# Router to first expert unit: normed tokens kept by feature column, their bf16 parts cut behind the first unit's columns, the gate row behind up

## The chip, the cores and the metric

The kernel runs on one core of a Trainium2 chip. The metric is the device time of one execution in microseconds (us). The engines named below are TensorE (PE: matmul; PEld: its weight loads), VectorE (DVE), ScalarE (ACT), GpSimd (POOL) and SyncE (SP), which here only issues DMA transfers. In tile names, `p_...` tiles lie in PSUM, the others in SBUF.

## The reference

Two transformer blocks on 256 tokens of 1024 features, one after the other, in float32. The place of the change is the mixture of experts at the end of the first block:

```python
h = rms_norm(x, g_ffn[l]) * (1.0 + scale_f) + shift_f
# hierarchical_moe(h): t = h as (256, 1024)
g_logits = t @ w_group + b_group                  # 4 groups
g_sel = argmax(g_logits)
e_logits = (t @ w_router[g_sel]) + b_router       # 8 experts of the chosen group
top_v, top_i = top_k(e_logits, 2)
w_top = softmax(top_v) * p_group
comb = sum(one_hot(eid, 32) * w_top)              # 256 x 32
hg, hu = t @ w_gate[e], t @ w_up[e]               # 32 experts, 1024 -> 256
y = sum over e of (silu(hg) * hu * comb[:, e]) @ w_down[e]
x = x + gate_f * y
```

## The kernel before, in words

The 256 tokens lie in two tiles t = 0, 1 of 128 partitions (`xt`, 1024 features each). Features are dealt out over partitions so that feature 8p + j belongs to column j; eight columns j = 0..7 make up one token.

The router (written out by hand, lines 1017 to 1050) goes tile by tile: `square` and `rstd` make 1/rms; `normed` (line 950) writes the normed tokens `xn2` (called `xn` in the profile) on ACT; `turned` copies the transposed tokens out of PSUM; `logits`, `groups` and `experts` find the two experts of each token (`selb`); `rank` and `places` count the tokens of an expert up to a slot number and make the 0/1 matrix `P0` (`P` in the profile). `gather_t` (line 998) then multiplies column j of `xn2` by `P0`, 8 float32 matmuls for each t, which moves the tokens of the first four experts into their slots (`p_xg`). Two kinds of order hold there: while the list `holding` is not empty, what goes through `held` keeps the order in which it is written, and with two entries so do matmuls. `warm(n)` issues n matmuls whose result nobody reads.

The 32 experts are worked off in 8 units of 4. A unit reads its gathered tokens `xg` (from `p_xg`, scaled on DVE and ACT by turns, `gather`, line 1059), multiplies by the gate and up weights (`gate_up`, `p_gu`), applies silu, and multiplies by the down weights (`p_dn`), which are scattered back (`p_sc`). While unit k runs, `prepare(k + 1)` gathers the tokens of the next one, in three bf16 parts instead of float32: `cut3` (line 1008) cuts the two tiles of `xn2` into `xn3` (also `xn` in the profile), with two ACT and two DVE passes over 1024 elements for each tile. `cut3` overwrites `xn2` on the way. Before the change these passes were not held: a scheduler places them.

`gate_row_end` (line 369) spreads one row over all partitions with two 512-wide matmuls (`p_row`); nobody needs it before the first unit's `p_dn` is read.

Expert weights, 1 MB each, come over SP's queue in a fixed order into rings of buffers (`load_experts`, line 228). `xn2` itself lies in the first of the five buffers of the ring `raw3`, so the load of that buffer's next owner, and all loads queued behind it, wait until `cut3` has read `xn2` for the last time:

```python
xn2 = raw3.tile([128, RAW], FT, name="xn2", tag="raw3")
```

Units 1 to 6 end in a branch (`branch`, `tc.If`, the profile's L1302) on the largest count of the unit; all engines pass through it, and SP's loads behind it are issued after it.

Of the kernel before, what the change touches and what calls it, by code (L numbers as in the profile page):

```python
# [11 lines left out]
AF = mybir.ActivationFunctionType  # L12
OP = mybir.AluOpType
# [19 lines left out]
def tile_block(ctx: ExitStack, tc: tile.TileContext, A, out):  # L33
    nc = tc.nc
    pe, act, dve, pool = nc.tensor, nc.scalar, nc.vector, nc.gpsimd
# [10 lines left out]
    def bank(shape, name):  # L46
        return ps.tile(shape, FT, name=name, tag="bank")
# [26 lines left out]
    holding = []  # L74

    def held(ins):

        if holding:
            tc.keep_in_program_order(ins)
        return ins  # L80
# [14 lines left out]
    def held_pe(ins):  # L95
        if len(holding) > 1:
            tc.keep_in_program_order(ins)

    def mm(o, lhsT, rhs, start, stop):
        held_pe(pe.matmul(o, lhsT, rhs, start=start, stop=stop, skip_group_check=True))  # L100

    def warm(n):

        if n:
            p = bank([128, 128], "p_warm")
            for _ in range(n):
                tc.keep_in_program_order(
                    pe.matmul(p, ident, ones, start=True, stop=True, skip_group_check=True))
# [27 lines left out]
    xt = const.tile([128, 2, D], FT, name="xt")  # L136
# [70 lines left out]
    for name in 'bq bq bk 2 2 bk bv bv 3 aq kv 2 2 3 3 aq 3 4 4 4 4 5 5 5 5'.split():  # L207
        if name == "kv":
            w_kv = load_cols("wkv", "w_in", WIN, 512, 256, 0, 8)
        elif name in COLS:  # L210
            c0, n = COLS[name]
            k = len(later[name])
# [156 lines left out]
    def gate_row_end():  # L369
        m = modrow[:, 1]  # L370
        b = [bank([128, 512], "p_row") for _ in range(2)]
        for half in range(2):
            mm(b[half], ones, m[:, 512 * half:512 * half + 512], True, True)
        for half in range(2):
            act.activation(m[:, 512 * half:512 * half + 512], b[half], AF.Copy)
# [75 lines left out]
    af = const.tile([128, 8], FT, name="af")  # L451
# [4 lines left out]
    bf_ = modcol[:, 2]  # L456
# [107 lines left out]
    def add_out(t, half):  # L564
        add_outs[0](t, half)
# [267 lines left out]
    st = proj_fm(w_iq, iqT, 1.0)  # L833
# [75 lines left out]
    xn2 = raw3.tile([128, RAW], FT, name="xn2", tag="raw3").rearrange("p (t d) -> p t d", t=2)  # L909
# [11 lines left out]
    rs2 = m1.tile([128, 2], FT, name="rs2")  # L921
# [7 lines left out]
    xn3 = m1.tile([128, 3, 2, 8, 128], BF, name="xn3")  # L929
# [13 lines left out]
    def rstd(t, step):  # L943
# [3 lines left out]
        else:  # L947
            held(dve.reciprocal(rs2[:, t:t + 1], ss2[:, t, 1:2]))

    def normed(t):  # L950
        held(act.activation(xn2[:, t], xt[:, t], AF.Copy, scale=rs2[:, t:t + 1]))

    def turned(t, half):
        if half:
            held(act.activation(xh[t][1], trb[t][1], AF.Copy))
        else:
            held(dve.tensor_copy(xh[t][0], trb[t][0]))
# [26 lines left out]
    def rank(t):  # L984
        if t:
            mm(pos_[:, 1], oneb, selb[:, 0], False, False)
        mm(pos_[:, t], trib, selb[:, t], t == 0, True)

    def places(t):
        held(dve.scalar_tensor_tensor(pos1[:, t], pos_[:, t], 1.0, selb[:, t], op0=OP.add, op1=OP.mult))  # L990
        held(dve.tensor_tensor(P0[:, t], iota1[:, None, 0:SLOTS].to_broadcast([128, 4, SLOTS]),
                               pos1[:, t, 0:4, None].to_broadcast([128, 4, SLOTS]), op=OP.is_equal))

    PP, XG = {}, {}
    P0f = P0.rearrange("p t e s -> p t (e s)")
    xgb = [bank([128, 4, 128], "p_xg") for _ in range(2)]

    def gather_t(t):
        for j in range(8):
            mm(xgb[j // 4][:, j % 4], xn2[:, t, j::8], P0f[:, t], t == 0 and j % 4 == 0, t == 1)  # L1000

    def gather_mm(u, banks, t):
        for j in range(8):
            for i in range(3):
                mm(banks[j // 4][:, j % 4], xn3[:, i, t, j], PP[u][:, t],
                   t == 0 and j % 4 == 0 and i == 0, t == 1 and i == 2)

    def cut3(src, parts):

        act.activation(parts[0], src, AF.Copy)  # L1010
        dve.tensor_tensor(src, src, parts[0], op=OP.subtract)
        act.activation(parts[1], src, AF.Copy)
        dve.tensor_tensor(parts[2], src, parts[1], op=OP.subtract)

    holding += [True, True]
    square(0, 0)
# [2 lines left out]
    rstd(0, 1)  # L1019
    add_out(1, 0)  # L1020
    turned(0, 0)
    normed(0)
    turned(0, 1)
    add_out(1, 1)
    logits(0)
    trb.append(turn_x(1))
# [11 lines left out]
    rank(0)  # L1038
    warm(3)
    places(0)  # L1040
    gather_t(0)
    warm(2)
    groups(1)
    experts(1)
    rank(1)
    places(1)
    warm(0)
    gather_t(1)
    del holding[:]
    def onehot(u, pos, slot):  # L1050

        n = pos.shape[2]
        P = m1.tile([128, 2, 4, SLOTS], BF, name="Pq", tag="Pq", bufs=3)[:, :, 0:n]
        for t in range(2):
            dve.tensor_tensor(P[:, t], slot[:, None, :].to_broadcast([128, n, SLOTS]),
                              pos[:, t, :, None].to_broadcast([128, n, SLOTS]), op=OP.is_equal)
        PP[u] = P.rearrange("p t e s -> p t (e s)")

    def gather(u, banks=None):

        n = 4 * SLOTS
        xg = m1.tile([128, 8, 128], FT, name="xg", tag="xg", bufs=XGB)[:, :, 0:n]
        if not banks:
            banks = [bank([128, 4, 128], "p_xg")[:, :, 0:n] for _ in range(2)]
            for t in range(2):
                gather_mm(u, banks, t)
        for jq in range(2):
            b = banks[jq]
            for jj in range(4):
                j = 4 * jq + jj  # L1070
                if jj % 2:
                    act.activation(xg[:, j], b[:, jj], AF.Identity, bias=bf_[:, j:j + 1], scale=af[:, j:j + 1])  # L1072
                else:
                    dve.tensor_scalar(xg[:, j], b[:, jj], af[:, j:j + 1], bf_[:, j:j + 1],  # L1074
                                      op0=OP.mult, op1=OP.add)
        XG[u] = xg

    gather(0, xgb)
    onehot(0, pos1[:, :, 0:4], iota1[:, 0:SLOTS])
    for t in range(2):  # L1080
        cut3(xn2[:, t].rearrange("p (n j) -> p j n", j=8), [xn3[:, i, t] for i in range(3)])


    p = bank([128, NEXP], "p_cnt")
# [41 lines left out]
    def gate_up(st, k):  # L1126
        if k == "g":
            st.b = bank([128, 512], "p_gu")
        o = 0 if k == "g" else 256
        for j in range(8):  # L1130
            for c, e in enumerate(st.es):
                s0 = SLOTS * c
                mm(st.b[SLOTS * c:SLOTS * c + SLOTS, o:o + 256], XG[st.u][:, j, s0:s0 + SLOTS], W[e, k][:, j],
                   j == 0 and o == 0, j == 7)
# [17 lines left out]
    def silu(st):  # L1152
        st.s = m1.tile([128, 256], FT, name="sl", tag="sl")
        act.activation(st.s[:st.n], st.b[:st.n, 0:256], AF.Silu)  # L1154
        dve.tensor_tensor(st.s[:st.n], st.s[:st.n], st.b[:st.n, 256:512], op=OP.mult)  # L1155
# [138 lines left out]
    def prepare(u):  # L1294
        es = ORDER[u]
        onehot(u, pos1[:, :, es[0]:es[0] + 4], iota1[:, 0:SLOTS])
        gather(u)
# [18 lines left out]
    for u, es in enumerate(ORDER):  # L1316
        st = Unit()
        st.u, st.es, st.n, st.y = u, es, SLOTS * len(es), {}
        units.append(st)
    for k, st in enumerate(units):  # L1320
        free = 0 < k < nu - 1
        n = len(st.es)
        gate_up(st, "g")
        if not free:
            load_experts(n)
        gate_up(st, "u")
        if not free:
            load_experts(n)
        silu(st)
        if k == 0:  # L1330
            gate_row_end()
        if k == 3:
            fallback()
        if k < nu - 1:
            prepare(k + 1)
        slots(st)
        turn(st)
        if st is not units[-1]:
            down(st)
            if not free:  # L1340
                load_experts(n)
            scatter(st)
            if free:
                branch(st)
                load_experts(3 * n)
        if k == 0:
            gr = modrow[0:24, 0, 0:128]
            for i, n in enumerate(("g_final", "mix_norm_w_2", "ffn_norm_w_2")):
                pool.dma_start(gr[8 * i:8 * i + 8], dram(n, 0, [[128, 8], [1, 128]]))
        if k == 2:  # L1350
            lb, oml, sp8 = constants2()
            p = bank([128, 24], "p_gg")
            pe.transpose(p, gr, ident[:24, :24])
            gcols = const.tile([128, 24], FT, name="gcols")
            dve.tensor_copy(gcols, p)
            gg = const.tile([128, 8], FT, name="gg")
            dve.tensor_mul(gg, gcols[:, 0:8], gcols[:, 8:16])
            nr = norm_row(0, "g_final")
        if 2 <= k <= 5:
            next(nr)  # L1360
# [62 lines left out]
    st = fm2(w_f, lambda b: fbanks.extend(b), (0,1,))  # L1423
# [27 lines left out]
    for fg in range(11):  # L1451
        src = [[2 * DFF, 128], [128 * 2 * DFF, 8], [1, 256]]
# [406 lines left out]
    st = gate_up2(0)  # L1859
# [53 lines left out]
    for half in range(2):  # L1913
# [10 lines left out]
                                  op0=OP.mult, op1=OP.mult))  # L1924
# [31 lines left out]
```

## Time and profile before

| | us |
|---|---|
| median of 3 runs (730.46 to 731.74) | 730.86 |
| the profiled execution's own time | 731.0 |
| its span, first to last instruction | 729.3 |
| PE busy / DVE busy / ACT busy | 661.0 / 400.2 / 303.5 |
| mean granted TensorE clock | 0.966 of full speed |

The profile records one execution. Some 1.7 us of its time lie outside the span. Times of rows are us from the start of the span. The router's last part and the first unit lie between 176 and 221 us, the eight units end at about 416 us, and the second block follows.

### The profile page before, as it was taken

The page shows a single profiled execution, that of the slowest core. Times are in us where ns is not written, and L with a number is a line of the kernel's source. Part 1 is how long each engine was busy: PE and PEld are TensorE (multiplying, and loading weights), DVE is VectorE, ACT ScalarE, POOL GpSimd, SP SyncE. Part 2 cuts the span into 40 slices and gives each one's busy share as a digit, 9 for nine tenths or more (in the row PEclk, how much of TensorE's full clock was granted, in tenths as well). Part 3 has the DMA queues.
Part 4 walks back from the last instruction along what each step waited for, and adds up shares of the span by engine and source line. Part 5 has one row for each costly group of instructions (what it writes and reads, how often), then busy time and mean ns, then how long its engine had stood idle before and what let it go on. Part 6 is the DMA issues. An engine that isn't in the chain of part 4 may idle for free. (4 is left out here: it accounts for less than half of the span.)

```text
span 729.3 us, 13242 instructions
## 1 busy us (share of the span) xinstructions
PE 661.0 (91%) x5489; PEld 511.3 (70%) x5489; DVE 400.2 (55%) x753; ACT 303.5 (42%) x505; POOL 46.1 (6%) x71
## 2 busy tenths in 40 slices
PE   4799999999899776898696999999999999999996
PEld 1498787677745524445252499987899999898994
DVE  2367967877653221323312378879576555555555
ACT  1446454754541101101110286775465444444445
POOL 7010000001000000000000153100000000000001
PEclk9899999999899998999987999999999999999998
DMA  9999669996469899998999999633535555550001
GB/s 343 372 381 375 233 262 337 378 420 218 175 273 421 328 417 416 359 423 328 421 421 412 372 364 391 220 117 116 174 116 175 196 200 196 172 202 17 1 1 58
DMA packets 69202, 196.93 MB, mean 270 GB/s; under 512 B 7550, under 2 KB 33219, under 8 KB 57350
## 3 DMA queue, kind: packets, MB, share of 16 engines
q1 hardware_dynamic: 67558, 195.30, 70.8%
q8 instruction: 53, 0.87, 0.5%
q10 hardware_dynamic: 1216, 0.30, 0.2%
q0 software_dynamic: 352, 0.28, 0.1%
q14 instruction: 23, 0.19, 0.1%
HBM read 194.81 MB, written 1.05 MB: 269 GB/s over the span
## 5 line engine op out<-in xcount | busy, mean ns | idle before, releaser
L100 PE MATMUL p_gu<-Xl,wguh 128*128 128x256 f32 x352 | 99.8, 284 | 0.0
L100 PE MATMUL p_gu<-Xh,wgul 128*128 128x256 f32 x352 | 99.3, 283 | 0.0
L100 PE MATMUL p_gu<-Xh,wguh 128*128 128x256 f32 x352 | 98.9, 283 | 0.1
L100 PEld LDWEIGHTS p_gu<-Xl,wguh 128*128 128x128 f32 x352 | 67.5, 192 | 0.5
L100 PEld LDWEIGHTS p_gu<-Xh,wguh 128*128 128x128 f32 x352 | 67.1, 192 | 0.7 <-ACT Xh L1385 0.4
L100 PEld LDWEIGHTS p_gu<-Xh,wgul 128*128 128x128 f32 x352 | 67.4, 192 | 0.3 <-DVE wgul L87 0.2
L100 PE MATMUL p_gu<-eg,xg 128*32 128x256 f32 x576 | 43.9, 434 | 16.6 <-PEq L1302 9.2
L100 PEld LDWEIGHTS p_gu<-eg,xg 128*32 128x32 f32 x576 | 21.1, 123 | 37.9 <-issue 26.8
L87 DVE TENSOR_TENSOR wdnl<-wdn,wdnh 128x1024 fp32r<-128x1024 f32 x22 | 27.0, 1225 | 32.4 <-ACT wdnh L86 32.4
L1155 DVE TENSOR_TENSOR sl<-sl,p_gu 128x256 f32<-128x256 f32 x9 | 3.8, 421 | 71.0 <-ACT sl L1154 71.0
L1154 ACT ACTIVATE sl<-p_gu 128x256 f32<-128x256 f32 x9 | 3.5, 383 | 89.4 <-PE p_gu L100 89.4
L100 PE MATMUL p_w<-hTh,wih 128*128 128x256 f32 x128 | 37.7, 298 | 2.5 <-ACT wih L86 2.5
L87 DVE TENSOR_TENSOR wgul<-wup,wguh 128x1024 fp32r<-128x1024 f32 x22 | 27.0, 1225 | 21.3 <-ACT wguh L86 20.2
L86 ACT ACTIVATE wdnh<-wdn 128x1024 fp32r<-128x1024 f32 x22 | 23.3, 1058 | 36.5 <-PE p_gu L100 35.9
L1072 ACT ACTIVATE xg<-p_xg,modcol,af 128x128 f32<-128x128 f32 x36 | 15.5, 460 | 54.1 <-DVE xg L1074 53.8
L87 DVE TENSOR_TENSOR wgul<-wgt,wguh 128x1024 fp32r<-128x1024 f32 x22 | 26.9, 1225 | 19.8 <-ACT wguh L86 19.8
L100 PE MATMUL p_dn<-ed,aT 128*32 128x512 f32 (+2 forms) x304 | 33.1, 573 | 4.9 <-ACT aT L1162 4.9
L100 PE MATMUL p_w<-Xh,w2h 128*128 128x256 f32 x128 | 37.0, 289 | 0.5 <-ACT w2h L86 0.3
L86 ACT ACTIVATE wguh<-wgt 128x1024 fp32r<-128x1024 f32 x22 | 23.3, 1061 | 33.7 <-PE p_gu L100 18.2
L100 PE MATMUL p_w<-hTl,wih 128*128 128x256 f32 x128 | 37.0, 290 | 0.0
L100 PE MATMUL p_w<-hTh,wil 128*128 128x256 f32 x128 | 36.7, 291 | 0.0
L100 PE MATMUL p_w<-Xh,w2l 128*128 128x256 f32 x128 | 36.1, 284 | 0.6 <-DVE w2l L87 0.6
(624 smaller groups left out, 1591.0 us busy)
## 6 DMA issues: line engine op xcount, KB each, us to landing
eg<-in_w_gate_dram SPq DMA_DIRECT2D x32, 1024.0 KB
eu<-in_w_up_dram SPq DMA_DIRECT2D x32, 1024.0 KB
ed<-in_w_down_dram SPq DMA_DIRECT2D x28, 1024.0 KB
wada<-in_w_ada_dram SPq DMA_DIRECT2D x24, 1024.0 KB
w<-in_w_in_dram SPq DMA_DIRECT2D x11, 1024.0 KB
wgt<-in_w_gate_up_dram SPq DMA_DIRECT2D x11, 1024.0 KB
wup<-in_w_gate_up_dram SPq DMA_DIRECT2D x11, 1024.0 KB
wdn<-in_w_down_dram SPq DMA_DIRECT2D x11, 1024.0 KB
```

The source lines that it names most:

```text
L86: held(act.activation(hi, src, AF.Copy))
L87: held(eng.tensor_tensor(lo, src, f32(hi), op=OP.subtract))
L100: held_pe(pe.matmul(o, lhsT, rhs, start=start, stop=stop, skip_group_check=True))
L1072: act.activation(xg[:, j], b[:, jj], AF.Identity, bias=bf_[:, j:j + 1], scale=af[:, j:j + 1])
L1154: act.activation(st.s[:st.n], st.b[:st.n, 0:256], AF.Silu)
L1155: dve.tensor_tensor(st.s[:st.n], st.s[:st.n], st.b[:st.n, 256:512], op=OP.mult)
```

## The change

The normed tokens are stored column by column: `xnj` is `xn2` seen as (t, j, n), and `normed` now reads `xt` with a step of 8 elements and writes each column in one piece. `gather_t` and `cut3` then read pieces without a step. `turned(0, 1)` goes ahead of `normed(0)`. `gather_t(0)` is split: columns 0 to 5 ahead of the second tile's group and expert choice, columns 6 and 7 behind its rank; the two `warm(2)` matmuls go (the third call issued none). The evictions `xg` are held in the order of j, and `cut3` is held behind them in two steps, over both tiles each. In unit 0, matmuls are held too, and `gate_row_end` goes behind the up product.

```diff
+    xnj = xn2.rearrange("p t (j n) -> p t j n", j=8)
+
     def normed(t):
-        held(act.activation(xn2[:, t], xt[:, t], AF.Copy, scale=rs2[:, t:t + 1]))
+        held(act.activation(xnj[:, t], xt[:, t].rearrange("p (n j) -> p j n", j=8), AF.Copy,
+                            scale=rs2[:, t:t + 1]))
-    def gather_t(t):
-        for j in range(8):
-            mm(xgb[j // 4][:, j % 4], xn2[:, t, j::8], P0f[:, t], t == 0 and j % 4 == 0, t == 1)
+    def gather_t(t, js):
+        for j in js:
+            mm(xgb[j // 4][:, j % 4], xnj[:, t, j], P0f[:, t], t == 0 and j % 4 == 0, t == 1)
-    def cut3(src, parts):
-        act.activation(parts[0], src, AF.Copy)
-        dve.tensor_tensor(src, src, parts[0], op=OP.subtract)
-        act.activation(parts[1], src, AF.Copy)
-        dve.tensor_tensor(parts[2], src, parts[1], op=OP.subtract)
+    def cut3(src, parts, step):
+        if step == 0:
+            held(act.activation(parts[0], src, AF.Copy))
+            held(dve.tensor_tensor(src, src, parts[0], op=OP.subtract))
+        else:
+            held(act.activation(parts[1], src, AF.Copy))
+            held(dve.tensor_tensor(parts[2], src, parts[1], op=OP.subtract))
...
     turned(0, 0)
+    turned(0, 1)
     normed(0)
-    turned(0, 1)
...
-    gather_t(0)
-    warm(2)
+    gather_t(0, range(6))
     groups(1)
     experts(1)
     rank(1)
+    gather_t(0, range(6, 8))
     places(1)
-    warm(0)
-    gather_t(1)
-    del holding[:]
+    gather_t(1, range(8))
...
     gather(0, xgb)
+    for step in range(2):
+        for t in range(2):
+            cut3(xnj[:, t], [xn3[:, i, t] for i in range(3)], step)
+    del holding[:]
     onehot(0, pos1[:, :, 0:4], iota1[:, 0:SLOTS])
-    for t in range(2):
-        cut3(xn2[:, t].rearrange("p (n j) -> p j n", j=8), [xn3[:, i, t] for i in range(3)])
...
+        if k == 0:
+            holding += [True, True]
         gate_up(st, "g")
...
         gate_up(st, "u")
...
-        silu(st)
         if k == 0:
             gate_row_end()
+            del holding[:]
+        silu(st)
```

In `gather`, the two eviction calls are wrapped in `held` and are otherwise as before.

The order on DVE at the second tile's expert choice, before (`selb` is the choice, `pos` and `P` the slots; `xn_1884` is `xn2`, `xn_1910` is `xn3`):

```order
L981 MATCH_REPLACE gone<-top_243,le_1897 128x32
L1011 TENSOR_TENSOR xn_1884<-xn_1884,xn_1910 128x8x128
L982 TENSOR_SCALAR selb<-gone 128x32
L990 SCALAR_TENSOR_TENSOR pos_1902<-p_pos,selb 128x32
L1088 COPY counts<-p_cnt 128x32
L991 TENSOR_TENSOR P_1914<-iota_1898,pos_1902 128x128
```

and after the change:

```order
L985 MATCH_REPLACE gone<-top_243,le_1897 128x32
L986 TENSOR_SCALAR selb<-gone 128x32
L994 SCALAR_TENSOR_TENSOR pos_1902<-p_pos,selb 128x32
L995 TENSOR_TENSOR P_1914<-iota_1898,pos_1902 128x128
```

The first pass of `cut3` no longer stands between the search and the choice. Where the passes stand now, on DVE, behind the evictions `xg` (`sl` is unit 0's silu product):

```order
L1080 TENSOR_SCALAR xg<-p_xg,af,modcol 128x128 x2
L1115 CAST comb_2058<-le_1897 128x64
L1116 TENSOR_TENSOR crest<-le_1897,comb_2058 128x64
L1080 TENSOR_SCALAR xg<-p_xg,af,modcol 128x128
L1117 CAST comb_2058<-crest 128x64
L1118 TENSOR_TENSOR comb_2058<-crest,comb_2058 128x64
L1016 TENSOR_TENSOR xn_1884<-xn_1884,xn_1910 128x1024 x2
L1019 TENSOR_TENSOR xn_1910<-xn_1884,xn_1910 128x1024 x2
L1164 TENSOR_TENSOR sl<-sl,p_gu 128x256
```

All four DVE passes follow one another between the last eviction and the silu product. On PE, from the first gather to the first unit, before:

```order
L100 MATMUL p_xg<-P_1914,xn_1884 128x128 x8
L108 MATMUL p_warm<-ones,ident 128x128 x2
...
L100 MATMUL p_pos<-selb,trib 128x32
L100 LDWEIGHTS oneb
L100 MATMUL p_cnt<-selb,oneb 128x32
L100 MATMUL p_xg<-P_1914,xn_1884 128x128 x8
L100 MATMUL p_gu<-eg,xg 32x256 x8
L100 MATMUL p_row<-modrow,ones 128x512 x2
L100 MATMUL p_gu<-eg,xg 32x256 x24
L100 MATMUL p_gu<-eu,xg 32x256 x32
```

and after:

```order
L100 MATMUL p_xg<-P_1914,xn_1884 128x128 x6
...
L100 MATMUL p_pos<-selb,trib 128x32
L100 MATMUL p_xg<-P_1914,xn_1884 128x128 x2
L100 LDWEIGHTS oneb
L100 MATMUL p_cnt<-selb,oneb 128x32
L100 MATMUL p_xg<-P_1914,xn_1884 128x128 x8
L100 MATMUL p_gu<-eg,xg 32x256 x32
L100 MATMUL p_gu<-eu,xg 32x256 x32
L100 MATMUL p_row<-modrow,ones 128x512 x2
```

Two of the first gather's products moved behind the rank, and the row's two products moved from inside the gate product to behind up. A float32 matmul of these rows stands in the profile as two instructions.

## Rows read from the trace of the kernel before

**Rows 1.** The page, part 2: mean DMA busy tenths, 40 slices of the span.
```profile
DMA  9999669996469899998999999633535555550001
```

**Rows 2.** Windows: stretch, us, busy of PE, PEld, DVE, ACT, POOL, PEclk, DMA, GB/s.
```profile
190.00:194.00 4.00, 2.18 (x15) 1.98 (x14) 2.21 (x4) 0.90 (x4) 0.00 (x0) 1.00 0.00 0
194.00:198.00 4.00, 3.46 (x14) 3.49 (x15) 3.30 (x9) 1.81 (x2) 0.00 (x0) 0.71 0.00 0
206.00:236.00 30.00, 28.83 (x386) 15.98 (x379) 10.19 (x24) 5.07 (x15) 0.00 (x0) 1.00 0.99 407
236.00:244.00 8.00, 4.92 (x38) 2.41 (x40) 3.56 (x7) 0.00 (x0) 0.00 (x0) 0.97 0.56 208
242.00:408.00 166.00, 132.49 (x1511) 70.17 (x1511) 40.86 (x86) 17.50 (x46) 1.02 (x2) 0.91 0.97 396
```

**Rows 3.** Waits of SP's queue: total us, times, longest us.
```profile
SPq L252 <- PEq L1302: 48.9, 4, 17.9
SPq L252 <- DVE xn L1013: 25.1, 1, 25.1
```

**Rows 4.** Timeline of SP: start, us, what.
```profile
205.46 1.94 SPq L252 DMA_DIRECT2D ed<-in_w_down_dram  x4
...
241.92 1.92 SPq L252 DMA_DIRECT2D ed<-in_w_down_dram  x3
```

**Rows 5.** Timeline of DVE and PE, second tile's choice and gather: idle in brackets.
```profile
189.49 0.18 DVE L981 MATCH_REPLACE8 gone<-top,le 128x32 f32<-128x32 f32 x1
...
191.52 2.00 DVE L1011 TENSOR_TENSOR xn<-xn,xn 128x1024 f32<-128x1024 f32 x1 [1.85 <-PE p_xg L100]
...
193.43 0.18 DVE L982 TENSOR_SCALAR selb<-gone 128x32 bf16<-128x32 f32 x1
...
194.10 0.29 DVE L991 TENSOR_TENSOR P<-iota,pos 128x128 f32<-128x128 f32 x1
...
194.54 4.17 PE L100 MATMUL p_xg<-P,xn 128*128 128x128 f32 x16 [0.68 <-DVE P L991]
```

**Rows 6.** Weight loads by tile (ns min/median/max), and a run of warm matmuls.
```profile
L100 PEld LDWEIGHTS p_xg<-P,xn x32: 313/336/341, 187.4 to 198.1; 128*128 128x128 f32 x32
...
L100 PEld LDWEIGHTS p_lg<-wr,h x32: 186/192/333, 179.3 to 186.4; 128*128 128x128 f32 x32
...
186.56 0.91 PE L108 MATMUL p_warm<-ones,ident 128*128 128x128 f32 x6
```

**Rows 7.** Lines by form, 160 to 212 us: count, busy us, mean ns.
```profile
L1010 ACT ACTIVATE xn<-xn 128x1024 bf16<-128x1024 f32 x2 | 4.2, 2094 | 0.0
L86 ACT ACTIVATE woh<-woa 128x1024 fp32r<-128x1024 f32 x3 | 3.2, 1064 | 3.6 <-PE p_wo L100 3.6
L951 ACT ACTIVATE xn<-xt,rs 128x1024 f32<-128x1024 f32 x2 | 2.3, 1142 | 0.2 <-DVE rs L948 0.2
...
L1013 DVE TENSOR_TENSOR xn<-xn,xn 128x1024 bf16<-128x1024 f32 x2 | 4.1, 2046 | 1.8 <-ACT xn L1012 1.8
L87 DVE TENSOR_TENSOR wol<-woa,woh 128x1024 fp32r<-128x1024 f32 x3 | 3.6, 1209 | 0.0
L1074 DVE TENSOR_SCALAR xg<-p_xg,af,modcol 128x128 f32<-128x128 f32 x5 | 1.9, 407 | 1.9 <-PE p_xg L100 1.9
```

**Rows 8.** Timeline, first unit: gate, row, up, next unit's gather.
```profile
198.64 1.27 PE L100 MATMUL p_gu<-eg,xg 128*32 128x256 f32 x16
...
199.84 1.98 PE L100 MATMUL p_row<-modrow,ones 128*128 128x512 f32 x4
...
203.60 2.37 PE L100 MATMUL p_gu<-eg,xg 128*32 128x256 f32 x40 [1.21 <-ACT xg L1072]
...
205.21 0.42 DVE L1103 SCALAR_TENSOR_TENSOR le<-le,w,selb 128x32 f32<-128x32 f32 x2
...
205.78 3.64 PE L100 MATMUL p_gu<-eu,xg 128*32 128x256 f32 x64
...
209.35 2.85 PE L100 MATMUL p_xg<-Pq,xn 128*128 128x128 bf16 x48
```

More of the change, by code (lines that the diff above doesn't have):

```diff
@@ L1071, in gather @@
                 if jj % 2:
-                    act.activation(xg[:, j], b[:, jj], AF.Identity, bias=bf_[:, j:j + 1], scale=af[:, j:j + 1])
-                else:
-                    dve.tensor_scalar(xg[:, j], b[:, jj], af[:, j:j + 1], bf_[:, j:j + 1],
-                                      op0=OP.mult, op1=OP.add)
+                    held(act.activation(xg[:, j], b[:, jj], AF.Identity, bias=bf_[:, j:j + 1],
+                                        scale=af[:, j:j + 1]))
+                else:
+                    held(dve.tensor_scalar(xg[:, j], b[:, jj], af[:, j:j + 1], bf_[:, j:j + 1],
+                                           op0=OP.mult, op1=OP.add))
         XG[u] = xg
     gather(0, xgb)
+    for step in range(2):
+        for t in range(2):
+            cut3(xnj[:, t], [xn3[:, i, t] for i in range(3)], step)
+    del holding[:]
     onehot(0, pos1[:, :, 0:4], iota1[:, 0:SLOTS])
-    for t in range(2):
-        cut3(xn2[:, t].rearrange("p (n j) -> p j n", j=8), [xn3[:, i, t] for i in range(3)])
     p = bank([128, NEXP], "p_cnt")
```

## The prediction

> **What bounds the kernel now.** I read the page's slices first. DMA falls to four tenths in the slice around 190 us [rows 1]; the windows resolve that: no byte moves from 190 to 198 us, the engine stays nearly fully supplied from 206 to 236, dips in 236 to 244, and runs at 0.97 over 242 to 408 [rows 2]. So the expert units are bound by transfers once they run, and the router's end is a stretch where transfers stand still. The waits of SP's queue say why: one wait of 25.1 us on DVE's L1013, the last pass that reads `xn2`, whose buffer the next load needs, and later waits on the branch L1302 [rows 3]. SP issues again at 205.46, and after the first unit's branch at 241.92 [rows 4]. The time in question is therefore the shift of that restart at 242: transfers are idle just ahead of it in either kernel, and what follows hangs on it.
>
> What sets 242? SP waits there for PE to arrive at the branch. From the second unit's gather at 209.35 to the branch PE runs 28.83 of 30 us [rows 2, 8], on weights that landed before 190 or come with the loads of 205. So the shift of the gather at 209.35 is the gain, as long as the transfers can follow: they restart at 205.46, and have 8 x (1 - 0.56) = 3.5 us of idle time to give ahead of 242 [rows 2, 4].
>
> **The change part by part.** Each step moves the start of that gather.
>
> (a) DVE. The search ends at 189.67, but `selb` starts at 193.43: the first `cut3` pass stands between, waits 1.85 us for PE to finish reading `xn2` (it overwrites it) and runs 2.00 [rows 5]. Now `selb` follows at once: -3.7 us. PE must be free for the rank at 189.9: the first gather starts at about 187.4, and six columns are 12 instructions; at 0.15 us (below) they end at 189.2, at the old 0.26 (4.17 / 16) at 190.5. With `P` 3.7 earlier, the second gather starts at 190.84 instead of 194.54.
>
> (b) The gather itself. Its 16 instructions took 4.10 us to the first `p_gu` at 198.64 [rows 5, 8]. Their weight loads, with a step of 8 elements, take 336 ns; those of `p_lg`, without one, 192; six warm matmuls of the same size run in 0.91, 0.15 each [rows 6]. I take 0.15 for loads without a step: 2.4 us, -1.7. Bounds: 0.26, no gain; and 0.12, an estimate for the warm run without the drain of its last product, 0.5 more. I take 0.15 because the warm run has the same form (128 x 128, float32, no step), and 192/336 of 0.26 is 0.15 too.
>
> [...]
>
> (c) The gate product. From the first `p_gu` to the next gather 10.71 us pass now [rows 8]; in them lie the row product, and waits for evictions that stand behind `cut3` passes on DVE and ACT. Steady `p_gu` needs 3.57 us for 64 instructions (205.78 to 209.35), 7.14 for gate and up. Now the evictions come first: column 0 starts at about 192.5, an estimate (its bank is complete at 192.05, eight instructions into the gather, and DVE has slot work of 0.2 us each until then), column 1 on ACT is ready by 193.4; before column 2 stand five small DVE operations at 0.2 us (0.42 for two), so it is ready at 194.3; the later ones, at 0.41 each and two pairs of small ones, keep ahead of PE's 0.45 a column. PE starts at 190.84 + 2.4 = 193.24, loses 0.2 to column 2, and ends up at 200.58. That is 7.34 instead of 10.71, -3.4.
>
> (d) The row product now adds to PE: four instructions, 199.84 to 201.75 before, where it lay in a wait [rows 8]: +1.9. The gather starts at 202.5.
>
> (e) `cut3`. Its last eviction is done at 196.0. Eight passes in pairs: with ACT at 1.06 and DVE at 1.21 (without a step) [rows 7], the chain ACT, DVE, ACT, DVE with the two tiles staggered ends at 201.9, 0.6 ahead of the gather: cost nothing while PE works through up and row. No row shows a bf16 pass without a step at this size; the other end is today's 2.05, which ends it at 206.3 (a rival). Silu's ACT work stands behind it, ready by 202, ahead of need.
>
> SP's load then goes out at 202.0, 3.5 us earlier. With the 3.5 us of idle time the transfers can follow 7.0.
>
> (f) `normed` reads with a step: from 1142 ns to at most 2094 [rows 7]. On ACT each of its two runs is followed today by a `cut3` pass of 2094 ns, which goes away there, so ACT is 1.1 us earlier behind each, not later. The tokens are first read at 187.4 and 190.8. Hidden, cost nothing; without that cover it would be 0.95 a tile on the second tile's path. `turned(0, 1)` moves ahead of it, on work that PE has finished: nothing.
>
> (g) The warm matmuls: PE would have waited there anyway; nothing, apart from the clock (a rival).
>
> Sum: -3.7 - 1.7 - 3.4 + 1.9 = -6.9 us. The profiled execution took 731.0 (its span 729.3 and 1.7 around it), so 724.1; the median of the runs is 0.14 below that execution, which gives 724.0. The likeliest case's own range is 1.2 either way: rank and eviction order by 0.3 each, the gather's speed by 0.6, and states of the clock further on.
>
> **The rivals.**
>
> *The gather does not run faster.* Then the rank waits for PE until 190.5, the second gather starts at about 191.7 and runs 4.1; `p_gu` finds its evictions ready, 7.14, row 1.9: the next gather at 204.85, gain 4.5, 726.4. For: p_lg's form differs. Against: [rows 6].
>
> [...]
>
> *`cut3` stays at 2.05 us a pass* because of bf16 and not the step. It ends at 206.3; the gather gains 3.0, SP's load goes out 0.9 us later than now, and the transfers gain 3.5 - 0.9 = 2.6: 728.3.
>
> *Slower: `cut3` in series.* If ACT and DVE did not overlap over the two tiles (held in order, at 2.05 us), eight passes end at 196.0 + 16.4 = 212.4. SP's load is then 6.9 us late; less the 3.5 of idle time the restart at 242 is 3.4 later: 734.3. It decides from an end of `cut3` at 209.0, 1.6 us a pass in series. Against: the passes of different tiles depend on nothing of each other.
>
> *Nothing.* The units are transfer-bound at 0.97; were the restart at 242 set by transfers already, or by something that does not move, the gain would be eaten: 730.9. Against: the 3.5 us of idle transfers.
>
> **How the numbers follow.** Forecast (-6.9) 0.58; slow gather 0.17; half clock 0.11; 2 us passes 0.06; series 0.03; nothing 0.05. Below 0.2% (1.5 us) a measurement of this kernel cannot be told from no change. The first four are faster by more: 0.92; nothing gives 0.04 same and a remnant of 0.01 on the slow side: slower 0.04, same 0.04. The range goes from the forecast's lower end, with 0.3 to spare, 722.5, over the half clock and the slow gather, with 1.1 us of tolerance for the latter, to 727.5; outside stay the last three rivals (0.14) and a little of the others.
>
> **What would show it.** Right: `selb` 0.2 us behind MATCH_REPLACE, `p_xg` pitch near 0.15 and its loads under 200 ns; `p_gu` without a break from 194.3; the row product at 200.6; `cut3` passes at 1.1 to 1.2 us; the ed load at 202; SP's restart at 235. Wrong: loads still at 336 ns; `p_xg` of the second unit waiting for DVE's last pass; PEclk at 0.5 between 193 and 200; a load queue that restarts at 235 but an end that has not moved by as much.

## The result, and the profile after

The changed kernel took 726.28 us (median of six runs, 723.59 to 726.91), beside 730.74 us (729.94 to 732.52) for the kernel before: a ratio of 0.993, 95% interval 0.9911 to 0.9949. That is 4.5 us gained where 6.9 were forecast; the time lies 2.3 us above the forecast and inside its range. The profiled execution took 726.6 us, its span 724.8.

Inside the router nearly every step came as forecast, some better. The timeline of the changed kernel from the second tile's choice to the second unit's gather (start, us, engine, line, operation; idle time before it in brackets) answers to [rows 5, 8]:

```profile
189.13 0.18 DVE L985 MATCH_REPLACE8 gone<-top,le 128x32 f32<-128x32 f32 x1
189.34 0.18 DVE L986 TENSOR_SCALAR selb<-gone 128x32 bf16<-128x32 f32 x1
190.02 0.29 DVE L995 TENSOR_TENSOR P<-iota,pos 128x128 f32<-128x128 f32 x1
...
190.46 2.02 PE L100 MATMUL p_xg<-P,xn 128*128 128x128 f32 x16
192.41 3.66 PE L100 MATMUL p_gu<-eg,xg 128*32 128x256 f32 x64
195.89 3.64 PE L100 MATMUL p_gu<-eu,xg 128*32 128x256 f32 x64
199.46 1.98 PE L100 MATMUL p_row<-modrow,ones 128*128 128x512 f32 x4
201.28 2.84 PE L100 MATMUL p_xg<-Pq,xn 128*128 128x128 bf16 x48
...
194.65 1.99 ACT L1015 ACTIVATE xn<-xn 128x1024 bf16<-128x1024 f32 x2
196.99 2.19 ACT L1018 ACTIVATE xn<-xn 128x1024 bf16<-128x1024 f32 x2 [0.34 <-DVE xn L1016]
...
198.08 2.36 DVE L1019 TENSOR_TENSOR xn<-xn,xn 128x1024 bf16<-128x1024 f32 x2
```

`selb` follows the search at once; the second tile's gather's 16 instructions take 2.02 us where [rows 5] show 4.17; gate and up run without a break; the last pass of the bf16 split ends at 200.44. The weight loads of the gather (ns, min/median/max), against 336 in [rows 6]:

```profile
L100 PEld LDWEIGHTS p_xg<-P,xn x32: 186/192/192, 187.1 to 192.1; 128*128 128x128 f32 x32
```

SyncE's timeline: the loads resume 4.87 us earlier than in [rows 4], and behind the first branch 6.64 earlier, at 235.28 as forecast:

```profile
200.59 2.72 SPq L252 DMA_DIRECT2D ed<-in_w_down_dram  x4
...
235.28 1.95 SPq L252 DMA_DIRECT2D ed<-in_w_down_dram  x3
```

The second unit's gather starts 8.1 us earlier than in [rows 8], 9.3 when both are counted from the router's first instruction (176.02 before, 177.24 after). At the start of block 2, the first transpose behind the experts, 4.4 us are left (416.22 before, 411.82 after); from there to the end both need 313 us. So the time is lost among the experts. The windows show where. First the changed kernel (stretch, us, busy time of PE, PEld, DVE, ACT, POOL, then PEclk, DMA share, GB/s):

```profile
192.00:200.00 8.00, 8.00 (x135) 4.65 (x134) 6.74 (x17) 6.53 (x9) 0.00 (x0) 1.00 0.01 2
200.00:208.00 8.00, 7.42 (x90) 4.50 (x92) 3.10 (x8) 4.05 (x10) 0.00 (x0) 1.00 0.77 261
232.00:244.00 12.00, 8.44 (x128) 4.86 (x128) 0.49 (x2) 0.00 (x0) 0.00 (x0) 0.86 0.94 370
292.00:308.00 16.00, 13.07 (x202) 7.31 (x204) 3.80 (x10) 2.76 (x7) 0.00 (x0) 1.00 0.73 287
324.00:344.00 20.00, 17.17 (x216) 9.25 (x217) 7.85 (x18) 3.43 (x10) 0.00 (x0) 1.00 0.84 332
```

and the kernel before over the last three stretches:

```profile
232.00:244.00 12.00, 8.93 (x70) 3.54 (x68) 4.74 (x8) 0.50 (x2) 0.00 (x0) 0.98 0.71 276
292.00:308.00 16.00, 14.59 (x198) 7.96 (x194) 5.88 (x13) 2.00 (x5) 0.00 (x0) 1.00 0.89 352
324.00:344.00 20.00, 17.30 (x214) 10.38 (x210) 6.78 (x14) 2.43 (x7) 0.00 (x0) 1.00 0.84 339
```

Length times (1 - share) is the time in which transfers stand still. They stand still three times behind their resuming. Stop 1, near 240 before and 236 after, shrank from 3.5 to 0.7 us, in the direction forecast. Stop 2, near 300, grew from 1.8 to 4.3. Stop 3 stayed at 3.2.

Units are counted from 0 here, so that the second unit is unit 1. At stops 1 and 3 SyncE waits for TensorE at a branch, 17.9 and 17.6 us before, of which the transfers already under way hide all but 3.5 and 3.2. Stop 2 is of another kind. Unit 3 has an expert with more than 32 tokens, so its branch is taken and an extra pass runs: the profile has nine silu products of expert units for eight units. SyncE must not load over the unit's weights before this pass has read them, and waits for its gate product (`p_gu`). SyncE's waits for `p_gu` in the kernel before (total us, times, longest us), then the first product of the extra pass before and after:

```profile
SPq L252 <- PE p_gu L100: 20.7, 4, 16.2
```

```profile
298.06 2.85 PE L100 MATMUL p_xg<-Pq,xn 128*128 128x128 bf16 x48 [1.27 <-DVE Pq L1055]
```

```profile
293.99 2.85 PE L100 MATMUL p_xg<-Pq,xn 128*128 128x128 bf16 x48 [1.27 <-DVE Pq L1060]
```

The longest of these waits is 16.2 us before and 19.2 in the changed kernel: TensorE begins the extra pass 4.1 us earlier, but the loads ahead of it were through earlier still.

What TensorE does ahead of stop 2 differs most at one place, the branch behind unit 2. The kernel before, then the changed one (timeline of TensorE; the p_gg product is the first behind the branch; in the brackets `PEq` and `DVEq` are the sequencers of TensorE and VectorE, and `issue` is a wait for nothing that the profile shows):

```profile
263.33 0.21 PE L1353 MATMUL p_gg<-ident,modrow 24*128 24x24 f32 x1 [0.99 <-DVEq L1302]
263.47 1.48 PE L100 MATMUL p_gu<-eg,xg 128*32 128x256 f32 x19
268.00 3.92 PE L100 MATMUL p_gu<-eg,xg 128*32 128x256 f32 x43 [3.05 <-issue]
```

```profile
259.86 0.27 PE L1365 MATMUL p_gg<-ident,modrow 24*128 24x24 f32 x1 [4.32 <-PEq L1311]
260.05 2.78 PE L100 MATMUL p_gu<-eg,xg 128*32 128x256 f32 x23
265.04 4.71 PE L100 MATMUL p_gu<-eg,xg 128*32 128x256 f32 x41 [2.20 <-issue]
```

TensorE waits 4.32 us there instead of 0.99, for its own sequencer, and stops again behind 23 instructions of the gate product instead of 19. The two matmuls that the change took away were four instructions, so the second stop comes at the same place of the instruction stream.

### The profile page after: what moved, and what is told of

Same layout as the page of the kernel before. It is cut to its first block, busy times and chain, and to the rows that moved or that the text cites. A ratio compares the mean times of both kernels' runs of the same rounds, so it can differ in the third digit from the quotient of the medians.

```text
span 724.8 us, 13236 instructions
## 1 busy us (share of the span) xinstructions
PE 656.0 (91%) x5485; PEld 504.5 (70%) x5485; DVE 397.1 (55%) x753; ACT 301.6 (42%) x505; POOL 46.7 (6%) x71
## 5 line engine op out<-in xcount | busy, mean ns | idle before, releaser
L100 PE MATMUL p_gu<-eg,xg 128*32 128x256 f32 x576 | 45.6, 450 | 15.3 <-PEq L1311 6.4
```

## The experiments

The theories, as the expectations name them. **A**: TensorE decides, and loses at the branches what it gained. **B**: the loads decide, one for one with the moment when SyncE resumes. **C**: the wait at a branch hangs on the place in TensorE's instruction stream; the changed kernel has two matmuls fewer ahead of the experts. **D**: it is chance. **E**, formed from the first eight runs, stands in an expectation below.

**Two matmuls back** (first, and once more beside other kernels).

```diff
     gather_t(0, range(6))
+    warm(2)
     groups(1)
```

> The changed kernel with two warm matmuls put back behind the first part of the gather, where TensorE waits 0.88 us for the rank of the second 128 tokens. The chain to the second unit's gather should stay (that gather at 201.3, SyncE's loads again at 200.6). Theory A (TensorE loses at the branches behind units 1 and 2 what it gained, because its instructions come late there, whatever they are): same as the changed kernel, 726.3, waits there 4.4 and 4.3 + 2.2. Theory B (the weight transfers decide, and they follow the moment when SyncE's loads resume): same, 726.3. Theory C (the waits at the branches hang on where the instruction stream lies; TensorE had as many instructions before as this kernel has again): waits back to 3.1 and 1.0 + 3.0, time about 722.5.

> The changed kernel with the two warm matmuls back, once more and beside other kernels, for the size of the gain: by the theory that has stood so far (E: from the router to the last expert the weight transfers run at full rate but for a few stops; a stop lasts from when SyncE has nothing it may load to when TensorE has passed the branch that SyncE too waits at; the wait of 4.3 us behind unit 2 lengthens the stop near 300) the short wait of 1.0 us comes again and the time is 2 to 3 us under the changed kernel, 0.989 of the kernel before. If the wait costs nothing: 0.993.

Measured: 725.12 us, ratio 0.9919 (0.9892 to 0.9946); 725.06, 0.9908 (0.9883 to 0.9932). In both profiles the wait is 0.99 again, and the next stop comes behind 19 instructions; TensorE's timeline of the first:

```profile
256.32 0.21 PE L1366 MATMUL p_gg<-ident,modrow 24*128 24x24 f32 x1 [0.99 <-DVEq L1312]
256.46 1.48 PE L100 MATMUL p_gu<-eg,xg 128*32 128x256 f32 x19
260.79 4.04 PE L100 MATMUL p_gu<-eg,xg 128*32 128x256 f32 x43 [2.85 <-issue]
```

The wait follows C, at this branch: at the one behind unit 1 C expected 3.1 us, and 4.27 and 4.31 came. The time went down by about 1 us and not by the 2 to 4 expected, and the intervals overlap with that of the changed kernel: what the wait costs is not settled by these two.

**Two matmuls less in the kernel before.**

```diff
-    warm(5)
+    warm(3)
```

> The kernel before with three warm matmuls instead of five ahead of the logits of the second 128 tokens: TensorE has two matmuls less, as the changed kernel has, and nothing else differs up to the branches. Theory C (place in the instruction stream): the wait at the branch behind unit 2 becomes 4.2 us and the next stop comes behind 23 gate matmuls instead of 19, as in the three kernels seen with that count; slower than the kernel before by 1.5 to 3 us (733). Theory D (chance, or the DMA traffic at that moment, which is that of the kernel before): the wait stays at 1.0 and the time at 731.

Measured: 732.85 us, 1.0016 (0.9998 to 1.0033), with this at the branch:

```profile
266.24 0.27 PE L1353 MATMUL p_gg<-ident,modrow 24*128 24x24 f32 x1 [4.95 <-PEq L1302]
266.44 2.78 PE L100 MATMUL p_gu<-eg,xg 128*32 128x256 f32 x23
```

The time is 2 us above the median of the kernel before (730.89 beside it), but the interval of the ratio still reaches below 1, so a loss is not clear of the noise. The place is shown: of the twelve profiles with these branches, the five with the count of the kernel before waited 0.99 each, the seven with two matmuls fewer 4.21 to 4.95. What makes the longer wait is not shown; as its end the profile names VectorE's sequencer in the five, and TensorE's own in the seven.

**The order without the layout.** The view `xnj` is made with feature = 8n + j, as the kernel before stores it, and `normed` writes as it did.

```diff
-    xnj = xn2.rearrange("p t (j n) -> p t j n", j=8)
+    xnj = xn2.rearrange("p t (n j) -> p t j n", j=8)
```

> The changed kernel's order, with the normed tokens stored as before (all readers stride by 8 again). The second gather should take about 4.2 us of 16 matmuls again or a little less, the xg evictions end near 196.5, and the bf16 split, at about 2.05 us a pass and behind those evictions, end near 206.7; SyncE's loads resume at 206.9, which is 1.4 us later than in the kernel before, and the second unit's gather starts at 206.7, 2.6 us earlier than before. Theory A (TensorE's gather counts, half of it given back at the branches): 729.4. Theory B (the loads' resuming counts): 732.

Measured: 731.79 us, 0.999 (0.997 to 1.0011). The new order alone brings nothing: loads resume at 207.46, later than in [rows 4]. The second unit's gather begins at 203.90, but with two instructions only; the rest waits for the split's passes until 205.40 and 207.36. This kernel too has the two matmuls fewer and waits 4.21 us behind unit 2, so the run does not part the order from that place.

**The layout without the order**: the kernel before, with `normed` writing and the gather and the split reading through the new `xnj`.

> The kernel before, with the normed tokens stored by feature column and nothing else of the change. The gather matmuls should go at a pitch of 0.12 us instead of 0.26, the split's passes at about 1.0 to 1.2 us instead of 2.05, so that SyncE's loads resume near 201.5 (205.46 before) and the second unit's gather comes near 205.5 (209.35 before; the gate row still stands inside the gate product). Theory A: half of the gather's 3.9 us is lost again, 728.8. Theory B: 4 us less, 726.9. If the layout carries nothing: 730.8.

Measured: 724.86 us, 0.9917 (0.9888 to 0.9945). The layout alone brings all that the whole change does, with a gather 3.5 us later than the changed kernel's (204.83); the intervals overlap. It has the matmul count of the kernel before. With that count the whole change took 0.9919 and 0.9908 (two matmuls back), the same within the noise: the order added nothing to be seen here. It keeps the short wait behind unit 2 (0.99), and the one behind unit 1 is 2.11 us instead of 4.44.

**The buffer freed later**, by five and by ten fills behind the split.

```diff
+    for r in range(5):
+        tc.keep_in_program_order(pool.memset(xn2[:, r % 2], 0.0))
```

> The changed kernel with five fills of the normed tokens' buffer by GpSimd (about 1 us each) behind the last pass of the bf16 split: nobody reads them, but the buffer, into which SyncE loads a piece of weights, comes free only after them. TensorE's work up to the second unit's gather stays (201.3); SyncE's loads resume near 205.4 instead of 200.6, as late as in the kernel before. Theory A (branches, not transfers): 726.3, as the changed kernel. Theory B (transfers): the gain is gone, 730.8. In between (the idle of the transfers near 232 to 236 takes it up, 0.7 us): 730.

> The changed kernel with ten fills of the normed tokens' buffer behind the split instead of the five of the kernel with the late buffer. By that one's 0.73 us a fill, SyncE's loads resume 7.3 us later than in the changed kernel, at about 206.5 from a router that starts at 176.0 (the kernel before: 205.5). TensorE up to the branch behind unit 1 stays as it was. Theory B (the time follows the loads' resuming, one for one): slower than the kernel before, 732 or more. Theory A (TensorE and its branches decide): 726.5. Half and half: 729.

Measured: five fills, loads at 202.96, 726.14 us, 0.9923 (0.99 to 0.9945); ten fills, loads at 208.75, 732.5, 1.0018 (1.0001 to 1.0035). With five fills the loads resume 2.4 us later in the trace, 3.6 counted from the router's start, and the median shows no loss, which speaks against B one for one; but the profiled execution itself was the slowest of its six, 728.41 us, 1.8 above the changed kernel's. A falls with the second: 8 us later loses the gain, with TensorE's gather where it was. Stop 1 is gone in both: the loads could come later by some us before it cost anything like their delay. How many is not measured between these two.

**TensorE later, the loads in time.**

```diff
+    for r in range(8):
+        tc.keep_in_program_order(pool.tensor_copy(xn3[:, 0, 0], xn3[:, 0, 0]))
```

(and TensorE's order held up to the first unit's scatter).

> The changed kernel with eight GpSimd passes (each copies the piece onto itself) over the first bf16 piece that the second unit's gather reads, and TensorE's order held through the first unit: SyncE's loads resume as in the changed kernel (23.4 us behind the router's start), but TensorE's second gather starts some 6 to 9 us later, about where it stands in the kernel before (33.3 behind the router's start). Theory A (TensorE's gather and the branches decide): the gain is gone, 730 to 732. Theory B (the loads decide): 726.5.

Measured: 731.66 us, 1.0015 (1.0001 to 1.0029). The gain is gone, though SyncE resumes at 200.55 as in the changed kernel. TensorE's waits, SyncE's loads behind the branch, and the windows:

```profile
206.88 5.30 PE L100 MATMUL p_xg<-Pq,xn 128*128 128x128 bf16 x48 [7.08 <-POOL xn L1091]
...
241.03 3.66 PE L100 MATMUL p_gu<-eg,xg 128*32 128x256 f32 x64 [1.91 <-PEq L1313]
```

```profile
200.55 2.02 SPq L252 DMA_DIRECT2D ed<-in_w_down_dram  x4
...
218.48 24.03 SPq L252 DMA_DIRECT2D ed<-in_w_down_dram  x4
```

```profile
232.00:244.00 12.00, 10.09 (x96) 4.45 (x92) 4.74 (x8) 0.49 (x2) 0.00 (x0) 1.00 0.43 155
```

The transfers ran dry and waited 6.8 us for TensorE to pass the branch. The waiting is 6.1 us more than the changed kernel's stop 1. So neither A nor B: both count, through the stops.

**The changed kernel once more.**

> The changed kernel once more, beside the kernels it is to be compared with. Theory C (the longer wait behind unit 2 hangs on where the instruction stream lies) expects the branch behind unit 2 to hold TensorE 4.2 us or more again, and the next stop behind 23 of the gate matmuls; theory D (it is chance, from run to run) leaves both 1.0 and 4.2 open. Time: 0.993 of the kernel before by the record; 726.3 to 727.2 beside a kernel before at 730.7 to 731.7.

Measured: 726.46 us, 0.9925 (0.9899 to 0.9951); the wait behind unit 2 is 4.33, the next stop behind 23 instructions again.

**Both kernels without the branches behind the middle units.** One line each, `branch(st)`, is left out, and with it the extra pass behind unit 3: these two have eight silu products of expert units, not nine.

> The changed kernel without the branches behind the six middle units (leaves out the pass that these would make for experts with more than 32 tokens; the one larger branch behind unit 3 stays). Theory E: neither TensorE nor SyncE stops there, the transfers lose nothing but the wait ahead of the router's buffer and what the branch behind unit 3 costs; about 6 us less than the changed kernel (720), and 5 to 6 us less than the kernel before without its branches, which is the difference of the loads' resuming (23.4 against 29.4 behind the router's start). Theory A (the branches took back what TensorE gained, and nothing else did): 9 us less than the kernel before without branches.

> The kernel before without the branches behind the six middle units (leaves out what the changed kernel without branches leaves out). Theory E: about 5 us less than the kernel before, 726, since its stops near 240, 304 and 340 took 3.5, 1.8 and 3.5 us of the transfers' time. Theory A: 8 us less or more, 722, since TensorE loses its waits of 3.1, 4.0 and 2 to 4 us at five branches.

Measured: the changed kernel 715.1 us (714.26 to 715.58), the kernel before 718.8 (718.38 to 719.68); 3.7 apart. The stops are gone; two windows of the kernel before without branches:

```profile
232.00:244.00 12.00, 12.00 (x132) 6.06 (x128) 6.22 (x13) 1.69 (x5) 0.00 (x0) 1.00 1.01 419
292.00:308.00 16.00, 15.42 (x203) 8.71 (x201) 5.12 (x12) 3.08 (x8) 0.00 (x0) 1.00 1.02 421
```

A's 9 falls; E's 5 to 6 is too much as well. The loads resume 4.3 us earlier in these two profiles, 2.8 when counted from the router's start, and block 2 starts 3.0 earlier; the medians' 3.7 lies between. Both kernels fell by more than E said, 11 and 12 us against 6 and 5: the stops alone are 8.2 and 8.5, and what is left besides (below) is 1.5 to 3.2 us shorter. Since the extra pass goes too, stop 2 ends here with the work and not only with the branch: what the branches alone cost is not parted from it.

**A version that beats both.** The row product and two split passes move into waits of the router; matmuls are filled up to the count of before.

```diff
-    warm(5)
+    row_mm(0)
+    warm(1)
     logits(1)
...
-    warm(3)
+    row_mm(1)
...
     gather_t(0, range(6))
+    warm(2)
```

(also four more warm matmuls ahead of the first logits, three behind the first unit's transposes; the first two ScalarE passes of the split ahead of `gather(0, xgb)`, the row's two evictions behind it.)

> The changed kernel with the gate row's product moved into TensorE's waits inside the router (in place of warm matmuls), the first two ScalarE passes of the split ahead of the gate columns, and as many warm matmuls as the kernel before had matmuls more, so that the branch behind unit 2 lies as it did there. The second gather should come at 22.3 us behind the router's start (24.0 in the changed kernel), SyncE's loads at 22.3 (23.4). Theory E: the branch behind unit 1 is passed 1.5 us earlier and the stop of the transfers ends as much earlier, 1 to 1.5 us below the kernel with the two warm matmuls, 0.988 of the kernel before. If only the loads counted: 1 us. If neither: 0.992.

Measured: 721.53 us (720.69 to 725.51), 0.9872 (0.9848 to 0.9896): faster than the changed kernel too, whose intervals (from 0.9911, and once more from 0.9899) lie wholly above. The gather comes at 198.38, 22.2 behind the router's start, and the loads resume 22.1 behind it. TensorE at the two branches, and the stops:

```profile
232.66 5.89 PE L100 MATMUL p_gu<-eg,xg 128*32 128x256 f32 x64 [4.39 <-DMA ed<-in_w_down_dram]
...
254.34 0.21 PE L1380 MATMUL p_gg<-ident,modrow 24*128 24x24 f32 x1 [0.99 <-DVEq L1325]
```

```profile
232.00:244.00 12.00, 11.34 (x165) 7.19 (x166) 0.42 (x1) 0.39 (x1) 0.00 (x0) 0.78 0.90 354
292.00:308.00 16.00, 14.35 (x175) 6.43 (x172) 4.27 (x9) 2.30 (x6) 0.00 (x0) 1.00 0.89 358
```

**All profiles in one balance.** Resume and gather as in the traces; stops from the windows 232 to 244, 292 to 308 and 324 to 344 as length times (1 - share), below zero set to zero; the last column is the start of block 2 less resume and stops. In two kernels stop 2 runs past 308: over 292 to 312 it is 6.2 us for order only and 4.8 for the kernel before with two less.

| kernel | loads resume | gather | wait, unit 1 / 2 | stops 1, 2, 3 | block 2 | rest |
|---|---|---|---|---|---|---|
| before | 205.46 | 209.35 | 3.08 / 0.99 | 3.5, 1.8, 3.2 | 416.22 | 202.3 |
| changed | 200.59 | 201.28 | 4.44 / 4.32 | 0.7, 4.3, 3.2 | 411.82 | 203.0 |
| changed, again | 200.27 | 200.96 | 4.33 / 4.33 | 1.4, 4.8, 3.6 | 412.01 | 201.9 |
| two matmuls back | 199.16 | 199.84 | 4.27 / 0.99 | 1.4, 2.4, 3.0 | 407.75 | 201.8 |
| the same again | 199.80 | 200.48 | 4.31 / 0.99 | 1.4, 4.0, 3.0 | 410.74 | 202.5 |
| order only | 207.46 | 203.90 | 4.22 / 4.21 | 0, 5.4, 3.2 | 418.97 | 202.9 |
| layout only | 199.88 | 204.83 | 2.11 / 0.99 | 3.4, 1.4, 3.2 | 409.55 | 201.7 |
| five fills | 202.96 | 200.01 | 4.49 / 4.27 | 0, 5.6, 3.4 | 413.00 | 201.0 |
| ten fills | 208.75 | 201.35 | 4.60 / 4.34 | 0, 2.6, 3.4 | 415.61 | 200.9 |
| TensorE later | 200.55 | 206.88 | 1.91 / 4.33 | 6.8, 3.2, 3.2 | 415.78 | 202.0 |
| before, two less | 204.32 | 208.24 | 3.18 / 4.95 | 3.5, 4.5, 3.4 | 418.30 | 202.6 |
| best | 198.24 | 198.38 | 4.39 / 0.99 | 1.2, 1.8, 3.2 | 406.64 | 202.2 |
| before, no branches | 204.62 | 208.53 | none | 0, 0, 0 | 403.70 | 199.1 |
| changed, no branches | 200.35 | 201.04 | none | 0, 0, 0 | 400.72 | 200.4 |

The start of block 2 moves over 18 us; the rest stays within 200.9 to 203.0 with branches, 199.1 and 200.4 without. That the table adds up says only that transfers run at one rate between the stops: a DMA share of 1.01 over 245 to 298 and 309 to 335 before (418 and 421 GB/s), and of 1.01 over 237 to 292 and 309 to 331 in the changed kernel (414 and 423). What tests theory E are the runs that moved the loads or TensorE alone, and there it holds (stop 1 at 6.8 us with TensorE later, at 0 with the fills): the experts take the time of their transfers, plus the resuming, plus the stops, and TensorE enters through the stops. Its wording needs a correction: stop 2 ends with the gate product of the extra pass, not with a branch.

Stop 2 is 1.4 to 1.8 in three of the kernels with the short wait, 2.4 and 4.0 in the other two; 4.3 to 5.6 with the long one, but 2.6 and 3.2 where TensorE or the loads came late. It follows TensorE's arrival: the start of the extra pass, less resume and stop 1, is 89.1 us before (298.06 - 205.46 - 3.5) and 92.7 in the changed kernel (293.99 - 200.59 - 0.7); less stop 2 as well it is 86.7 to 88.4 in all twelve profiles. So the long wait lengthens stop 2 as far as it makes TensorE late, and that is not a fixed amount: behind the short wait TensorE then waits for unit 3's up weights, 0.49 us before, 0 and 2.72 with the two matmuls back, 1.86 with the layout alone, 1.85 in the best; behind the long one it never does.

The two profiles with the matmuls put back are one kernel: stop 2 took 2.4 us in an execution of 723.26 us and 4.0 in one of 725.5. Unit 3's up product in each, the first without a wait, the second with two:

```profile
264.67 3.83 PE L100 MATMUL p_gu<-eu,xg 128*32 128x256 f32 x62
```

```profile
262.93 0.62 PE L100 MATMUL p_gu<-eu,xg 128*32 128x256 f32 x2 [0.86 <-DMA eu<-in_w_up_dram]
265.41 5.28 PE L100 MATMUL p_gu<-eu,xg 128*32 128x256 f32 x58 [1.86 <-DMA eu<-in_w_up_dram]
```

The granted clock over 264 to 268 was 1.00 in the first; in the second it was 0.67 there and 0.91 over 268 to 272, and the extra pass began 91.2 and 92.6 us behind the resuming: that is the difference, in these two. What makes it in other runs has no trace; the changed kernel's twelve runs scatter alike: three lie at 723.1 to 723.6, the others at 725.8 to 727.4.

## Why the prediction was right, and where it was wrong

The steps inside the router:

- (a) `selb` at once behind the search: as forecast (0.21 us behind it).
- (b) The gather: 1.95 us to the first `p_gu`, 2.15 less, where 1.7 were forecast. The pitch is 0.12 us, the lower of the two bounds, and the loads take 192 ns, 336 before, for the same 128 columns of the same product; 192 is what `p_lg`'s took, whose products have 36 columns and not 128. It goes with the step and not with the order: the first gather's 16 instructions took 4.08 us before and 2.05 with the layout only, the second's 4.17 before and 4.05 with the order only. That ends the first rival.
- (c) Gate and up: 7.05 us, 7.34 forecast.
- (d) The row product: 1.82 us on TensorE, as forecast, but more than half hidden behind the split. Without it, by an estimate from these rows, the gather would have waited for the split's end at 200.44 and gained 0.8 us, not 1.9. The best version, which takes it away and brings the split forward too, gains 1.8.
- (e) The split: 1.04 to 1.22 us a pass and an end at 200.44, 1.5 earlier than worked out; both rivals about it fall.
- (f) `normed` with a step: 2152 ns, 58 ns above the bound, and hidden.
- (g) The clock: the half clock that the chances and the range count in did not come: the granted clock was 1.00 over 192 to 200 us in all ten profiles with the new order. No run shows what it would have cost the gate product in this order: its chance of 0.11 and its place in the range were the author's estimate. What the runs show: in the kernel before the granted clock was 0.50 over 196 to 198, and 0.81 over the first 1.20 us of the gate product; with the layout only it was 0.57 over 192 to 196, and the second gather's 16 instructions took 3.63 us there, where those of the changed kernel took 2.02 at 1.00. Ahead of the gate product, over 182 to 186 us, it differs from one execution to another: PEclk 0.57 before, 1.00 in the changed kernel's first profile, 0.69 in its second, with the same ten warm instructions in 2.35, 1.28 and 2.34 us. The windows of the changed kernel's two profiles:

```profile
182.00:186.00 4.00, 4.00 (x38) 4.00 (x37) 2.73 (x14) 3.27 (x7) 0.00 (x0) 1.00 1.01 426
```

```profile
182.00:186.00 4.00, 4.00 (x28) 4.00 (x28) 1.37 (x8) 3.98 (x3) 0.00 (x0) 0.69 1.01 426
```

This matters for the sum. Counted from the router's start, the gather stands at 33.33 (before) and 25.60 (changed) in the profiles with a granted clock of 0.57 and 0.69 over 182 to 186, and at 31.64 (before with two less; without branches 31.66) and 24.04 (changed) in those with 1.00. Like against like it came 7.7 or 7.6 us earlier, 6.9 forecast; the loads' resuming came 4.5 or 4.4 earlier, 3.5 forecast. The 9.3 of the two first profiles mixes the clocks.

The step that failed: "So the shift of the gather at 209.35 is the gain, as long as the transfers can follow." The transfers followed to the branch: resumed 4.9 earlier, and stop 1 2.8 shorter. The step took what comes behind it as fixed, and it was not: stop 2, set by an extra pass that the prediction does not name, grew by 2.5 us. In the balance, 4.9 + 2.8 - 2.5 = 5.2, against 4.4 seen at block 2 and 4.5 in the span; the other 0.8 is the last column's 203.0 against 202.3 and rounding, and has no cause shown. Ahead of that stop TensorE waited 3.3 us more at the branch behind unit 2, since two matmuls less, costed at "nothing" as filler, had moved the code behind it. That the place makes the wait is shown on both kernels; that the stop follows TensorE's arrival is shown in all twelve profiles; what the wait costs in the median is not settled, since the runs with the matmuls put back gained about 1 us and not 2.5.

A second thing the sum did not see: the loads behind a branch wait not only for TensorE's arrival but for the branch itself. Before, SyncE issued 2.8 us behind the end of TensorE's last product ahead of the branch behind unit 1 (239.12 to 241.92), and in the changed kernel 4.2 us behind it (231.12 to 235.28). Ahead of stop 1 the gain at the gather was cut by this: TensorE reached the branch behind unit 1 earlier, while transfers still ran (a DMA share of 0.94 over its wait, 0.13 before), and waited there 4.44 us instead of 3.08.

One of the prediction's own signs of being wrong came: a load queue that restarts at 235 with an end that has not moved by as much, 6.64 us against 4.5. And that the time lies in the range is in part luck: 726.28 falls on the price of the rival with the slow gather, 726.4, whose condition did not come, and which had set the range's upper end.

The rival "nothing" was nearer than its chance of 0.05 said, in kind: the experts are bound by transfers (a DMA share of 1.01 between the stops), and a good part of what TensorE gains comes to nothing (8.1 us at the gather, 4.4 at block 2). It was wrong that the resuming would not move.

## What to carry to other kernels

Where a stage is bound by transfers, count the moments in which transfers stand still, and what ends each; here 8.1 us gained at TensorE's gather left 4.4 at block 2. A change that takes instructions away ahead of a branch can lengthen the wait behind it (here from 0.99 us to 4.32): compare the wait at every later branch, and keep the instruction count when testing a part. See in the profile which branches are taken, and what the work behind them holds back. Before crediting a new order, try its data layout alone; here that was the whole gain of the change (724.86 us against 726.28).

## What the runs showed of the hardware

- The wait at the branch behind unit 1 goes with the transfers that run meanwhile. The windows of exactly that wait in the layout-only kernel and in the one with five fills:

```profile
234.61:236.72 2.11, 0.00 (x1) 0.03 (x1) 1.18 (x3) 0.00 (x0) 0.00 (x0) 0.99 0.06 23
```

```profile
229.86:234.35 4.49, 0.00 (x0) 0.03 (x1) 1.18 (x3) 0.00 (x0) 0.00 (x0) 0.90 1.02 418
```

  Over twelve profiles: 1.91 to 3.18 us at DMA shares of 0.00 to 0.13, 4.22 to 4.60 at 0.79 to 1.02. This is a correlation; no run moved the transfers alone at that place. In four of the eight long ones (changed, the same again, the second with the two matmuls back, best) the profile names the landing of a load (`ed`) as what ended the wait, and not TensorE's sequencer, so that part of it may be a wait for weights; in the other four, 4.22 to 4.60 us long, it names the sequencer. What makes the sequencer wait is not shown.
- The scatter from run to run is smaller where the branches, and with them the extra pass, are left out: six runs of the changed kernel spread over 3.3 us, six more over 4.3, five without branches over 1.3; the kernel before over 2.6 in six runs, without branches over 1.3 in five.
- A float32 weight load of 128 columns (the gather's) with a step of 8 elements took 336 ns, without 192; a ScalarE pass of 1024 elements (the split's first) 2.09 us against 1.04, a VectorE pass (its last) 2.05 against 1.22, each before against after.
